# Layer 1 of a two-layer decoder on one core: the second half's norms made without GpSimd and over a longer stretch, its keys and values one group of heads later, the last output weights split once

## The chip, the cores and the metric

The kernel runs on one core of a Trainium2 chip. The metric is device time in microseconds (us), one whole execution of the program. Three runs of the kernel before gave 984.8 to 984.9, median 984.82 us.

A core has TensorE (PE, the matmuls; its weight loads are shown apart as PEld), VectorE (DVE), ScalarE (ACT), GpSimd (POOL) and SyncE (SP), which here only issues transfers. Each engine runs its own instructions in its own order and waits for the others by semaphores.

## The reference

Sequence 1024, width 1024, batch 1, all in float32. Layer 0 is a gated pooling mixer, which the change leaves alone. Layer 1 is attention in a sliding window of 128 positions, with 16 heads of 64 and two key/value heads; cut to what matters:

```python
shift, scale, gate = split(c_act @ ada_w + ada_b, 3)
hk = modulate(rmsnorm(x, kv_norm_g), kv_shift, kv_scale)   # norm for keys and values
kv = hk @ w_kv
h  = modulate(rmsnorm(x, norm_g), shift, scale)            # norm for queries and gates
q, z = split(h @ w_in, 2)
# 128 queries against 256 keys (the block before and their own)
s = q*64**-0.5 @ k + pos_bias ; s = where(band mask, s, -1e30)
m = maximum(max(s), sink) ; p = exp(s - m)
p = p / (sum(p) + exp(sink - m)) ; o = p @ v
x = x + gate * ((o * silu(z)) @ w_out)
return rmsnorm(x, final_g)
```

with `modulate(h, shift, scale) = h * (1 + scale) + shift`.

## The kernel before

**Numbers.** A float32 product is made of three matmul passes on a faster 32-bit type: each operand is split into a high part (a cast) and a low part (value minus high part), and PE adds hi x hi, lo x hi and hi x lo (lines L203 to L205). A tile of weights, 128x1024 values in 512 KB, is loaded on SP's queue into `raw`, cast by ScalarE (`wh`, L121) and subtracted by VectorE (`wl`, L123).

**Layout.** The activations `x` stay in SBUF as eight tiles (k = 0 to 7) of 128 features by 1024 positions. Everything of layer 1 is done for the first half of the positions (q = 0, 512 columns) and then for the second (q = 1). The 16 heads are four groups of four (r = 0 to 3).

**One block.** `attend(q, r, b)` handles 128 positions of one group; this is called a block here, and there are 32. In order: scores on PE into `ps_S`; VectorE copies the key-mask part (L1107), adds the bias and takes the maximum (L1111), ScalarE takes the exponential (L1115), VectorE the reciprocal `den` (L1118) and the division of `pt` (L1119); PE transposes `pt` into `ps_tp` (L1125); ScalarE and VectorE split the result into `cur` (VectorE's part is L1129); GpSimd makes `prev` (L1134) and `cur` (L1137) out of it by masking; PE multiplies with the values into `ps_o` (L1148, L1149); ScalarE's `ol` and VectorE's `of` (L1155) join its halves, VectorE multiplies the gate `szb` in (`of`, L1159), and ScalarE and VectorE (L1161) split the product into the tile `qt`, in the place where the queries were.

**The other work of a group.** `project` makes the queries (`qt`, VectorE's part L1063) and the gates (`szb`, L1077) of a group with four tiles of weights. `keys` and `values` make half a sequence's keys and values, `values_split` brings the values into position-major tiles. `out_part` multiplies one half of the heads with output weights `wbo` and adds the result to `x` (L686); after the second half of the heads the squares for the final norm are summed (`sqh`, the additions on GpSimd). For the last quarter of the work (second half of the positions, second half of the heads) `out_quarter` reads output weights that are already split: `load_last` loads four tiles, casts them on ScalarE (L1223) and takes the low part on GpSimd (L1224). The same four tiles were loaded and split in the usual way for the first half of the positions as well.

**Norms.** A norm is eight tiles of 128x512, each made as high and low part. The norms of the first half (before these stretches) use `fold_h` and `fold_l`: VectorE multiplies `x` by scale and by the row `rb` in one instruction (L892), ScalarE adds the shift and casts (`hm`), VectorE adds the shift and subtracts the high part in one instruction (L898). The norms of the second half, `hk1` for keys and values and `h11` for queries and gates, are made by `prepare` while the first half's blocks run: VectorE multiplies `x` by `rb` (`xn`, L177), ScalarE makes the high part (L159), ScalarE makes the modulated value again in full precision (L163), GpSimd subtracts (L167).

**Order.** PE's order is written out by hand. `specs` is a list of steps; a planner keeps a `clock` that grows with the cost of each matmul step, and a list of events (the parts of `attend`, the tiles of a norm, the final pass). An event is put into the program as soon as the clock has passed its due time. The due times come from the numbers `GAPS` (between blocks), `FIRST`, `LAGS` (within a block), `PREP` (between tiles of a norm) and `FINISH`. VectorE, ScalarE and GpSimd get their order from a scheduler that starts from this program order. Weights are loaded one step ahead of their use.

Of the kernel before, what the change touches and what calls it, by code (L numbers as in the profile page):

```python
# [33 lines left out]
LAGS = (6.0, 6.0)  # L34
GAPS = (6.9, 6.9, 6.6, 6.6, 6.6, 6.6, 6.6, 6.6)
FIRST = 3.2
PREP = (2.6, 4.0, 2.5)
FINISH = (1.0, 0.5)


# [15 lines left out]
def trunk(ctx, tc, xT, c, pack, ada_first, ada_rest, wu0_in, wg0_in, wa, wg, wao, wkv,  # L56
# [24 lines left out]
    def half(q):  # L81
        return slice(q * H, (q + 1) * H)
# [67 lines left out]
    def rstd_spread(rs, n):  # L150
# [3 lines left out]
            mm(bc[:, j * P:(j + 1) * P], rs[:, j:j + 1].broadcast_to([P, P]), ident,  # L154
               start=True, stop=True)
        return bc

    def mod_h(xn, a, b, h):
        nc.scalar.activation(h, xn, AF.Identity, bias=b, scale=a)  # L159

    def mod_l(xn, a, b, h, l, f_eng=None, l_eng=None):
        if f_eng is nc.scalar:
            nc.scalar.activation(xn, xn, AF.Identity, bias=b, scale=a)  # L163
        else:
            nc.vector.tensor_scalar(out=xn, in0=xn, scalar1=a, scalar2=b,
                                    op0=ALU.mult, op1=ALU.add)
        (l_eng or nc.gpsimd).tensor_sub(out=l, in0=xn, in1=h.bitcast(F32))  # L167

    def split_mod(xn, a, b, h, l, f_eng=None):

        mod_h(xn, a, b, h)
        mod_l(xn, a, b, h, l, f_eng)

    def xn_tile(k, q, rb, xn=None):
        if xn is None:
            xn = sp.tile([P, H], F32, tag="xn", name="xn", bufs=5)
        nc.vector.tensor_mul(out=xn, in0=xk[k][:, half(q)], in1=rb)  # L177
        return xn

    sqh = [None, None]  # L180

# [36 lines left out]
    with ExitStack() as sa:  # L218
# [658 lines left out]
        class Modulated:  # L877


            act = False  # L880

            def __init__(self, q, rb, a0, shift):
                self.q, self.rb, self.a0, self.shift, self.tiles = q, rb, a0, shift, []
                self.xn = {}
# [14 lines left out]
                    out=self.tiles[k // 2][:, k % 2, 1, :], in0=self.xn.pop(k), scalar=b,  # L899
                    in1=h.bitcast(F32), op0=ALU.add, op1=ALU.subtract)  # L900

            def step(self, k):
                self.step_h(k)
                self.step_l(k)

            def args(self, k):
                a, b = self.a0 + k, self.shift + k
                return acol[:, a:a + 1], adac[:, b:b + 1], self.tiles[k // 2][:, k % 2, 0, :]

            def step_h(self, k, xn=None):  # L910
                if k % 2 == 0:
                    self.tiles.append(hp.tile([P, 2, 2, H], F32R, tag="h", name="hm"))
                self.xn[k] = xn_tile(k, self.q, self.rb, xn)
                mod_h(self.xn[k], *self.args(k))

            def step_l(self, k, l_eng=None):
                mod_l(self.xn.pop(k), *self.args(k), self.tiles[k // 2][:, k % 2, 1, :],
                      nc.scalar if self.act else None,
                      l_eng)

            def __call__(self, k, i, q=0):
                return self.tiles[k // 2][:, k % 2, i, :]
# [91 lines left out]
    def keys(q, hk, ps=None):  # L1014
        def done(ps):
            cols = half(q)
            for kv in range(2):
                a, b = slice(kv * 64, kv * 64 + 64), slice((1 - kv) * 64, (1 - kv) * 64 + 64)
                nc.scalar.copy(out=KH[kv][a, cols], in_=ps[a, :])
                nc.scalar.copy(out=KH[kv][b, cols], in_=ps[a, :])  # L1020
                hs = KH[kv][a, cols].bitcast(F32)
                nc.vector.tensor_sub(out=KL[kv][a, cols], in0=ps[a, :], in1=hs)
                nc.vector.tensor_sub(out=KL[kv][b, cols], in0=ps[a, :], in1=hs)
        if ps is not None:
            return done(ps)
        return wkv[0], lambda w: gemm_steps(w, 0, hk, KT, done)
# [3 lines left out]
    def values(q, hk, ps=None):  # L1030
        def done(ps):
            vts[q] = bp.tile([P, H], F32, tag="ol", name="vt", bufs=1)
            nc.scalar.copy(out=vts[q], in_=ps)
        if ps is not None:
            return done(ps)
        return wkv[1], lambda w: gemm_steps(w, 0, hk, KT, done)

    def values_split(q):
        def run(w):
            ps = bank("d")  # L1040
            for j in range(4):
                nc.tensor.transpose(ps[:, j * P:(j + 1) * P], vts[q][:, j * P:(j + 1) * P], ident)
            pv = ps.rearrange("p (s c) -> p s c", c=64)
            vh, vl = VS[:, q * 8:q * 8 + 8, 0, :], VS[:, q * 8:q * 8 + 8, 1, :]
            nc.scalar.copy(out=vh, in_=pv)
            nc.vector.tensor_sub(out=vl, in0=pv, in1=vh.bitcast(F32))
            yield 0.43
        return None, run
# [3 lines left out]
    def queries(q, r, j, h1):  # L1052
        def run(w):
            if j == 0:
                pool, tag, bufs = (bp, "q2", 2) if r < 2 else (hp, "h", 8)
                qts[q, r] = pool.tile([P, 2, 2, H], F32R, tag=tag, name="qt", bufs=bufs)
            qt = qts[q, r]

            def done(ps):
                for e in range(2):  # L1060
                    a, b = slice(e * 64, e * 64 + 64), slice((1 - e) * 64, (1 - e) * 64 + 64)
                    nc.scalar.activation(qt[a, j, e, :], ps[a, :], AF.Copy, scale=0.125)
                    nc.vector.scalar_tensor_tensor(  # L1063
                        out=qt[b, j, e, :], in0=ps[a, :], scalar=0.125,
                        in1=qt[a, j, e, :].bitcast(F32), op0=ALU.mult, op1=ALU.subtract)
            yield from gemm_steps(w, 0, h1, KT, done)
        return wb[2 * r + j], run
# [98 lines left out]
    def out_part(q, part, n2):  # L1166

        def run(w):
            acts = lambda k, i: qts[q, 2 * part + k // 2][:, k % 2, i, :]
            for i in range(2):  # L1170
                n = 2 * n2 + i

                def done(ps):
                    residual(n, q, ps, 40)
                    if part == 1:
                        square_add(n, q, nc.gpsimd)
                yield from gemm_steps(w, i * 512, acts, 4, done)
        return wbo[part, n2], run

    def bare(f):  # L1180
        def run(w):
            f()
            yield 0.1
        return None, run
# [30 lines left out]

    last_w = []

    def load_last():

        raw = wp.tile([P, 1024], F32, tag="raw", name="raw")  # L1220
        nc.sync.dma_start(raw, wbo[1, len(last_w)])
        w = hp.tile([P, 2, T], F32R, tag="h", name="wo")
        nc.scalar.copy(out=w[:, 0, :], in_=raw)  # L1223
        nc.gpsimd.tensor_sub(out=w[:, 1, :], in0=raw, in1=w[:, 0, :].bitcast(F32))  # L1224
        last_w.append((w[:, 0, :], w[:, 1, :]))

    def stats_quarter(c):
        def f():
# [36 lines left out]
    def stats(q):  # L1265
        def f():
            state["rs"] = rstd_stats(sqh[q], 4)
        return bare(f)
# [34 lines left out]
    def prepare(m, ks, gap):  # L1303

        def gen():
            if m.rb is None:
                m.rb, m.act = state["rb"], True
            for k in ks:
                m.step(k)
                yield gap  # L1310

        return bare(lambda: push(clock[0], gen()))
# [9 lines left out]
    def project(q, r, h1, gap, after_first=()):  # L1322
        return [queries(q, r, 0, h1), *after_first, queries(q, r, 1, h1), start(q, r, gap),
                gates(q, r, 0, h1), gates(q, r, 1, h1)]

    def project_out(q, part):
        return [ready(q, part)] + [out_part(q, part, n2) for n2 in range(4)]

    def woven(l, at):

        r = []
        for i, x in enumerate(l):
            r.append(x)
            if i in at:
                r.append(bare(load_last))
        return r

    keys(0, hk0, got["pswk"])
    values(0, hk0, got["pswv"])
    specs = [  # L1340
        *project(0, 0, h10, GAPS[0], [values_split(0), stats(1)]),
        bare(norm_second), prepare(hk1, range(8), PREP[0]),
        *project(0, 1, h10, GAPS[1]),
        keys(1, hk1), values(1, hk1),
        *project(0, 2, h10, GAPS[2], [values_split(1)]),
        prepare(h11, range(4), PREP[1]),
        *project(0, 3, h10, GAPS[3]),
        prepare(h11, range(4, 8), PREP[2]),
        *project_out(0, 0),
        *project(1, 0, h11, GAPS[4]),  # L1350
        *project(1, 1, h11, GAPS[5]),
        *project(1, 2, h11, GAPS[6]),
        *project(1, 3, h11, GAPS[7]),
        *woven(project_out(0, 1) + project_out(1, 0)[:2], (0, 2, 4, 6)),
        stats(0), project_out(1, 0)[2], finish(0, 4, FINISH[0]),
        *project_out(1, 0)[3:],
        ready(1, 1),
        *[out_quarter(0, n2) for n2 in range(4)],
        out_quarter(1, 0), stats_quarter(0), out_quarter(1, 1), finish(H, 2, FINISH[1]),
# [3 lines left out]
    with tc.manual_schedule(engines={mybir.EngineType.PE}):  # L1363
        srcs = [i for i, sp_ in enumerate(specs) if sp_[0] is not None]
        loaded = {srcs[0]: got["wq"]}
        for i, (src, run) in enumerate(specs):
            if src is not None:
                nxt = srcs.index(i) + 1
                if nxt < len(srcs):
                    loaded[srcs[nxt]] = load_w(specs[srcs[nxt]][0])  # L1370
            for cost in run(loaded.pop(i, None)):
                clock[0] += cost
                while events and events[0][0] <= clock[0]:
                    advance()
        while events:
            advance()
# [55 lines left out]
```

## Time and profile before

| profiled execution | |
|---|---|
| its own time, span | 984.87 us, 982.6 us |
| instructions | 12696 |
| mean granted TensorE clock | 0.996 |
| PE | 961.9 us busy, 98% of the span |
| PEld | 801.2 us, 82% |
| VectorE | 775.7 us, 79% |
| ScalarE | 458.1 us, 47% |
| GpSimd | 145.0 us, 15% |
| HBM read, written | 111.22 MB, 13.63 MB |

The span is the time from the first to the last instruction of the profiled execution, 2.3 us less than the execution's own time. PE's load of weights overlaps its matmuls, so the two shares don't add. Layer 1 with the attention runs from about 616 us to the end; the blocks of the first half of the positions and the norms of the second half lie between about 630 and 752 us.

### The profile page before, as it was taken

Reading aid. Unit: us, or ns where it says so; the run is one execution under the profiler, and the core shown is the slowest. Engines: PE = TensorE matmul, PEld = TensorE weight load, DVE = VectorE, ACT = ScalarE, POOL = GpSimd, SP = SyncE. Lnnn points to the kernel's source line nnn. Section 1 sums busy time; section 2 is a strip of 40 time slices with the busy share of each in tenths; the row PEclk is TensorE's granted clock in tenths of the full one; section 3 lists DMA queues with packets and bytes.
Section 4 is the critical chain, followed back from the end, with each engine's and each line's share of the span. In section 5 each row is a group of like instructions: output and inputs, shape, how many; then the busy total and the mean of one; then the engine's idle time right before and its main releaser. Section 6 shows DMA issues by size and latency. Waiting matters only on the chain.

```text
span 982.6 us, 12696 instructions
## 1 busy us (share of the span) xinstructions
PE 961.9 (98%) x4538; PEld 801.2 (82%) x4538; DVE 775.7 (79%) x1411; ACT 458.1 (47%) x902; POOL 145.0 (15%) x173
## 2 busy tenths in 40 slices
PE   8999999999999999999999999999999999999996
PEld 6788888888888887888888888877888888887786
DVE  5897978677978699676782278599899878889985
ACT  6534434333433244551111145486677546566544
POOL 2100000000000000000000000052324313335723
PEclk9999999999999999999999999999999999999998
DMA  9453622264225411779861223222211221223222
GB/s 331 183 174 114 192 103 65 78 201 150 65 85 194 150 64 57 262 267 327 305 216 65 86 64 130 86 65 69 82 66 64 87 86 65 64 88 106 86 87 86
DMA packets 40625, 125.67 MB, mean 128 GB/s; under 512 B 4465, under 2 KB 6641, under 8 KB 40434
## 3 DMA queue, kind: packets, MB, share of 16 engines
q1 hardware_dynamic: 40416, 123.82, 37.6%
q10 hardware_dynamic: 146, 1.05, 0.3%
q8 instruction: 35, 0.57, 0.2%
q14 instruction: 28, 0.23, 0.1%
HBM read 111.22 MB, written 13.63 MB: 127 GB/s over the span
## 4 chain that ended last, share of the span: by engine, by line
PE 78%; DVE 16%; issue 2%; ACT 2%; POOL 1%; DMA 0%; POOLq 0%; DVEq 0%; SPq 0%; ACTq 0%
PE ps_d L214 14%; PE ps_S L214 9%; PE ps_d L636 9%; PE ps_d L203 6%; PE ps_d L204 6%; PE ps_d L205 6%; PE ps_S L636 4%; PE ps_o L214 4%; PE ps_tp L214 3%; DVE wl L123 2%; PE ps_d L374 2%; PE ps_o L636 2%; PE ps_tp L636 2%; DVE tmp L542 2%; PE ps_tp L1125 1%
## 5 line engine op out<-in xcount | busy, mean ns | idle before, releaser
L121 ACT CAST wh<-raw 128x1024 fp32r<-128x1024 f32 x73 | 76.5, 1048 | 101.4 <-PE ps_d L214 78.5
L123 DVE TENSOR_TENSOR wl<-raw,wh 128x1024 fp32r<-128x1024 f32 x73 | 94.2, 1290 | 26.7 <-ACT wh L121 22.8
L203 PE MATMUL ps_d<-hm,wh 128*128 128x512 f32 x288 | 113.8, 395 | 0.0
L205 PE MATMUL ps_d<-hm,wl 128*128 128x512 f32 x288 | 112.4, 390 | 0.3 <-DVE wl L123 0.3
L204 PE MATMUL ps_d<-hm,wh 128*128 128x512 f32 x288 | 112.4, 390 | 0.0
L239 DVE CUSTOM_DVE_ANT_0 tmp<-tmp,cact,pk 128x1024 f32<-128x1024 f32 x48 | 60.7, 1282 | 33.2 <-DMA tmp<-ada_rest 32.9
L214 PE MATMUL ps_d<-gh,wh 128*128 128x512 f32 x224 | 82.0, 389 | 0.0
L214 PE MATMUL ps_S<-gh,wh 128*128 128x512 f32 x192 | 64.5, 390 | 0.0
L205 PEld LDWEIGHTS ps_d<-hm,wl 128*128 128x128 f32 x288 | 54.1, 188 | 12.6 <-DVE wl L123 1.1
L636 PE MATMUL ps_d<-hs,ws 128*128 128x512 f32 x264 | 63.4, 389 | 0.0
L1115 ACT ACTIVATE pt<-pt,nm 128x129 f32<-128x129 f32 x128 | 50.2, 394 | 26.8 <-DVE nm L1111 24.6
L203 PEld LDWEIGHTS ps_d<-hm,wh 128*128 128x128 f32 x288 | 54.1, 188 | 10.2
L204 PEld LDWEIGHTS ps_d<-hm,wh 128*128 128x128 f32 x288 | 54.2, 188 | 10.0
L636 PEld LDWEIGHTS ps_d<-hs,ws 128*128 128x128 f32 x264 | 49.5, 188 | 10.3
L542 DVE TENSOR_TENSOR tmp<-tmp 128x1039 f32<-128x1039 f32 (+3 forms) x40 | 49.4, 1235 | 6.8 <-ACT tmp L672 5.7
L612 ACT CAST ws<-tw 128x512 fp32r<-128x512 f32 x44 | 26.8, 621 | 53.9 <-PE ps_tp L214 15.1
L636 PE MATMUL ps_d<-ha,ws 128*128 128x512 f32 x216 | 51.9, 389 | 0.0
L534 POOL MEMSET tmp<- 128x16 f32 x16 | 1.7, 111 | 331.4 <-DVE tmp L542 115.9
L214 PEld LDWEIGHTS ps_d<-gh,wh 128*128 128x128 f32 x224 | 42.1, 188 | 8.7
L636 PEld LDWEIGHTS ps_d<-ha,ws 128*128 128x128 f32 x216 | 40.5, 188 | 8.4
L147 POOL TENSOR_TENSOR rs<-v,mhalf 128x4 f32<-128x4 f32 (+1 forms) x7 | 8.2, 1164 | 241.6 <-DVE v L145 241.6
L214 PE MATMUL ps_d<-gh,wl 128*128 128x512 f32 x112 | 43.6, 389 | 0.0
(294 smaller groups left out, 2492.0 us busy)
## 6 DMA issues: line engine op xcount, KB each, us to landing
tmp<-ada_rest SPq DMA_DIRECT2D x48, 512.0 KB, 4.7
raw<-wb SPq DMA_DIRECT2D x32, 512.0 KB, 3.3
raw<-wa SPq DMA_DIRECT2D x28, 512.0 KB, 3.7
raw<-wao SPq DMA_DIRECT2D x20, 512.0 KB, 4.1
ad<-ada_first SPq DMA_DIRECT2D x16, 512.0 KB, 5.0
x<-xT SPq DMA_DIRECT2D x32, 256.0 KB, 5.9
raw<-wbo SPq DMA_DIRECT2D x16, 512.0 KB, 3.3
kept_g<-tmp SPq DMA_DIRECT2D x14, 512.0 KB, 2.9
```

The costliest lines, as they stand in the source:

```text
L121: nc.scalar.copy(out=wh, in_=raw)
L123: nc.vector.tensor_sub(out=wl, in0=raw, in1=wh.bitcast(F32))
L203: mm(ps, lh, acts(k, 0), start=k == 0, stop=False)
L204: mm(ps, lh, acts(k, 1), start=False, stop=False)
L205: mm(ps, ll, acts(k, 0), start=False, stop=k == n - 1)
L214: mm(p, lhs, acts(k, hl, q), start=start and k == 0 and s == 0, stop=stop and k == n - 1 and s == 2)
L239: nc.vector.tensor_tensor_reduce(out=raw, in0=raw, in1=ca, scale=0.5, scalar=pk[:, bcol:bcol + 1], op0=ALU.mult, op1=ALU.add, accum_out=ad ...
L374: mm(psu[i, q], w0[k // 2][:, k % 2, w, i * P:(i + 1) * P], block(k, q)[hl], start=k == 0 and s == 0, stop=k == KT - 1 and s == 2)
L542: nc.vector.tensor_add(out=nx[:, 2 * s - 1:], in0=cur[:, 2 * s - 1:], in1=cur[:, s - 1:PAD + T - s])
L612: nc.scalar.copy(out=ws[i][:, 0, :], in_=src)
L636: mm(ps, lhs, acts(k, hl), start=start and k == 0 and s == 0, stop=k == 3 and s == 2, skip_group_check=True)
L1115: nc.scalar.activation(pt[:, i, :P + 1], pt[:, i, :P + 1], AF.Exp, bias=nm[:, i:i + 1], scale=-1.0, accum_out=den[:, i:i + 1])
```

## The change

It has four parts.

1. `prepare` uses `fold_h` and `fold_l` for `hk1` and `h11`: two VectorE instructions and one ScalarE instruction a tile, instead of one of VectorE, two of ScalarE and one of GpSimd. The 16 tiles of the two norms are spread further apart: `PREP` goes from (2.6, 4.0, 2.5) to (4.8, 4.2, 4.2) us, and `h11` is cut into tiles 0 to 5 and 6 to 7 instead of 0 to 3 and 4 to 7.
2. `keys(1)` and `values(1)` stand behind the projection of group 2 and no longer ahead of it, `values_split(1)` in the projection of group 3. The pool `q2` has three buffers, and the queries of the first half's group 2 lie in it rather than in `h`.
3. `load_last` goes. The second set of output weights is loaded and split once (`load_any`, VectorE's subtraction L1188), for the first half of the positions, and kept for `out_quarter`. Sixteen loads of output weights become twelve.
4. The order of the late steps: the first tile of the second half's first output projection comes ahead of the first half's second output projection (before: behind it), `stats(0)` behind the second of these tiles (before: the first) and `finish` of the first half behind the third (before: the second).

```diff
-PREP = (2.6, 4.0, 2.5)
+PREP = (4.8, 4.2, 4.2)
...
     def queries(q, r, j, h1):
-                pool, tag, bufs = (bp, "q2", 2) if r < 2 else (hp, "h", 8)
+                pool, tag, bufs = (bp, "q2", 3) if r < 2 + (q == 0) else (hp, "h", 8)
...
-    def load_last():
-
-        raw = wp.tile([P, 1024], F32, tag="raw", name="raw")
-        nc.sync.dma_start(raw, wbo[1, len(last_w)])
+    def load_any(src):
+
+        if not isinstance(src, tuple):
+            return load_w(src)
+        raw, = fetch(wbo[src])
+        if src[0] == 0:
+            return split_w(raw)
         w = hp.tile([P, 2, T], F32R, tag="h", name="wo")
         nc.scalar.copy(out=w[:, 0, :], in_=raw)
-        nc.gpsimd.tensor_sub(out=w[:, 1, :], in0=raw, in1=w[:, 0, :].bitcast(F32))
+        nc.vector.tensor_sub(out=w[:, 1, :], in0=raw, in1=w[:, 0, :].bitcast(F32))
         last_w.append((w[:, 0, :], w[:, 1, :]))
+        return last_w[-1]
...
     def prepare(m, ks, gap):
             for k in ks:
-                m.step(k)
+                m.fold_h(k, sp.tile([P, H], F32, tag="xn", name="xn", bufs=5))
+                m.fold_l(k)
                 yield gap
...
         *project(0, 1, h10, GAPS[1]),
+        *project(0, 2, h10, GAPS[2]),
         keys(1, hk1), values(1, hk1),
-        *project(0, 2, h10, GAPS[2], [values_split(1)]),
-        prepare(h11, range(4), PREP[1]),
-        *project(0, 3, h10, GAPS[3]),
-        prepare(h11, range(4, 8), PREP[2]),
+        prepare(h11, range(6), PREP[1]),
+        *project(0, 3, h10, GAPS[3], [values_split(1)]),
+        prepare(h11, range(6, 8), PREP[2]),
...
-        *woven(project_out(0, 1) + project_out(1, 0)[:2], (0, 2, 4, 6)),
-        stats(0), project_out(1, 0)[2], finish(0, 4, FINISH[0]),
-        *project_out(1, 0)[3:],
+        *project_out(1, 0)[:2],
+        *project_out(0, 1),
+        project_out(1, 0)[2], stats(0), project_out(1, 0)[3], finish(0, 4, FINISH[0]),
+        project_out(1, 0)[4],
```

Three places show how the instructions stand on their engines. In the rows stand line, operation, output and inputs, and shape; a row that occurs several times in a stretch has xN. Lines behind the change are some 40 lower.

VectorE at the second block of the first half, where the norm `hk1` begins; before, then after:

```order
L1118 RECIPROCAL den<-den 128x4
L177 TENSOR_TENSOR xn<-x,rb_4917 128x512
L1119 TENSOR_TENSOR pt<-pt,den 128x4x128
L177 TENSOR_TENSOR xn<-x,rb_4917 128x512 x4
L1063 SCALAR_TENSOR_TENSOR qt<-ps_d,qt 64x512
L177 TENSOR_TENSOR xn<-x,rb_4917 128x512 x2
L123 TENSOR_TENSOR wl<-raw,wh 128x1024
```

```order
L1079 RECIPROCAL den<-den 128x4
L868 SCALAR_TENSOR_TENSOR xn<-x,acol,rb_4917 128x512
L1080 TENSOR_TENSOR pt<-pt,den 128x4x128
L868 SCALAR_TENSOR_TENSOR xn<-x,acol,rb_4917 128x512
L874 SCALAR_TENSOR_TENSOR hm<-xn,adac,hm 128x512
L868 SCALAR_TENSOR_TENSOR xn<-x,acol,rb_4917 128x512
L874 SCALAR_TENSOR_TENSOR hm<-xn,adac,hm 128x512
L123 TENSOR_TENSOR wl<-raw,wh 128x1024
```

Seven multiplies stood between the first division and the next split; now five folds stand there, three first folds (L868) and two second folds (L874), and the other tiles follow in later blocks.

VectorE at the end of a block while the norm `h11` is made: `of` joins and gates a block's output, `cur` is the split that GpSimd's masks start from, `qt` the split of the gated output; before, then after:

```order
L1155 SCALAR_TENSOR_TENSOR of<-ps_o,ol 64x256 x2
L1129 TENSOR_TENSOR cur<-ps_tp,cur 128x512
L1159 TENSOR_TENSOR of<-of,szb 128x256
L1107 COPY_PREDICATED ps_S<-tri,ps_S 128x2x128 x2
L1161 TENSOR_TENSOR qt<-of,qt 128x2x128
```

```order
L1116 SCALAR_TENSOR_TENSOR of<-ps_o,ol 64x256 x2
L1090 TENSOR_TENSOR cur<-ps_tp,cur 128x512
L1120 TENSOR_TENSOR of<-of,szb 128x256
L874 SCALAR_TENSOR_TENSOR hm<-xn,adac,hm 128x512
L1122 TENSOR_TENSOR qt<-of,qt 128x2x128
```

A second fold (L874) now stands right behind the gated `of`, ahead of the split into `qt`.

VectorE late in the second half, where the kept output weights are split; before, then after:

```order
L1129 TENSOR_TENSOR cur<-ps_tp,cur 128x512
L1118 RECIPROCAL den<-den 128x4
L1119 TENSOR_TENSOR pt<-pt,den 128x4x128
L123 TENSOR_TENSOR wl<-raw,wh 128x1024
L1077 SCALAR_TENSOR_TENSOR szb<-szb,ps_d 128x512
```

```order
L1090 TENSOR_TENSOR cur<-ps_tp,cur 128x512
L1188 TENSOR_TENSOR wo<-raw,wo 128x1024
L1079 RECIPROCAL den<-den 128x4
L1038 SCALAR_TENSOR_TENSOR szb<-szb,ps_d 128x512
L1080 TENSOR_TENSOR pt<-pt,den 128x4x128
L123 TENSOR_TENSOR wl<-raw,wh 128x1024
```

The first of the four kept splits (L1188) and the gate row (`szb`) moved ahead of the block's division.

More of the change, by code (lines that the diff above doesn't have):

```diff
@@ L156, in rstd_spread @@
         return bc
[L158 to L178, printed above, removed]
     sqh = [None, None]
@@ L877, in trunk @@
         class Modulated:
-            act = False
             def __init__(self, q, rb, a0, shift):
@@ L900, in fold_l @@
                     in1=h.bitcast(F32), op0=ALU.add, op1=ALU.subtract)
-            def step(self, k):
-                self.step_h(k)
-                self.step_l(k)
             def args(self, k):
@@ L908, in args @@
                 return acol[:, a:a + 1], adac[:, b:b + 1], self.tiles[k // 2][:, k % 2, 0, :]
[L910 to L919, printed above, removed]
             def __call__(self, k, i, q=0):
@@ L1177, in run @@
                 yield from gemm_steps(w, i * 512, acts, 4, done)
-        return wbo[part, n2], run
+        return (part, n2), run
     def bare(f):
@@ L1306, in gen @@
             if m.rb is None:
-                m.rb, m.act = state["rb"], True
+                m.rb = state["rb"]
             for k in ks:
-                m.step(k)
+                m.fold_h(k, sp.tile([P, H], F32, tag="xn", name="xn", bufs=5))
+                m.fold_l(k)
                 yield gap
@@ L1327, in project_out @@
         return [ready(q, part)] + [out_part(q, part, n2) for n2 in range(4)]
[L1329 to L1336, printed above, removed]
     keys(0, hk0, got["pswk"])
@@ L1369, in trunk @@
                 if nxt < len(srcs):
-                    loaded[srcs[nxt]] = load_w(specs[srcs[nxt]][0])
+                    loaded[srcs[nxt]] = load_any(specs[srcs[nxt]][0])
             for cost in run(loaded.pop(i, None)):
```

## Prediction

> **What bounds the kernel now.** I read the page first, then the waits of TensorE, then busy time by stretch, then the rows round each stall. On the page:
>
> ```profile
> span 982.6 us, 12696 instructions
> PE 961.9 (98%) x4538; PEld 801.2 (82%) x4538; DVE 775.7 (79%) x1411; ACT 458.1 (47%) x902; POOL 145.0 (15%) x173
> ```
>
> TensorE is busy for 98% of the span, and the change removes no matmul: its order on PE has the same instructions, some shifted by a few places. What can be won is PE's idle time in layer 1. The waits of PE at 600 to 760 us and at 870 to 945 us (in all, times, longest), two answers:
>
> ```profile
> PE ps_tp L1125 <- DVE pt L1119: 3.8, 3, 1.6
> ...
> PE ps_tp L1125 <- DVE pt L1119: 2.3, 2, 1.5
> PE ps_tp L154 <- DVE cur L1129: 0.4, 1, 0.4
> ```
>
> Nearly all of it is one wait: the transposes of the probabilities (L1125) wait for VectorE's division of them (L1119). Busy time by stretch (PE, PEld, DVE, ACT, POOL, granted clock, DMA share, GB/s):
>
> ```profile
> 616.00:945.00 329.00, 321.72 (x1612) 269.21 (x1611) 287.55 (x687) 207.27 (x495) 122.26 (x114) 1.00 0.24 78
> 641.00:752.00 111.00, 106.80 (x533) 88.60 (x532) 102.89 (x247) 84.99 (x192) 48.54 (x45) 1.00 0.22 71
> 645.00:669.00 24.00, 20.75 (x108) 17.16 (x105) 23.61 (x49) 20.94 (x44) 16.15 (x14) 1.00 0.21 67
> 760.00:860.00 100.00, 100.00 (x500) 84.42 (x499) 82.91 (x208) 56.43 (x143) 26.00 (x30) 1.00 0.23 74
> 878.00:934.00 56.00, 53.19 (x270) 43.92 (x269) 52.16 (x112) 32.94 (x78) 38.06 (x30) 1.00 0.30 95
> ```
>
> Over all heads PE is idle 329.0 - 321.7 = 7.3 us: 4.2 in the first stretch (641 to 752, where the second half's norms run), 2.8 in the second (878 to 934, where the output weights are split), none in the quiet 760 to 860. Even a change that cured everything would win about 7.3 us, 0.7%. PE stalls where VectorE is full: at 645 to 669 us it is idle 0.4 us of 24.
>
> **How far VectorE is ahead.** The division and the transposes after it, at the second block of heads (641) and where the two stretches end and begin:
>
> ```profile
> 640.48 0.68 DVE L1119 TENSOR_TENSOR pt<-pt,den 128x512 f32<-128x512 f32 x1
> 644.74 0.27 PE L1125 MATMUL ps_tp<-ident,pt 128*128 128x128 f32 x1
> 655.50 0.68 DVE L1119 TENSOR_TENSOR pt<-pt,den 128x512 f32<-128x512 f32 x1
> 656.33 0.63 PE L1125 MATMUL ps_tp<-ident,pt 128*128 128x128 f32 x4 [1.60 <-DVE pt L1119]
> 752.88 0.27 PE L1125 MATMUL ps_tp<-ident,pt 128*128 128x128 f32 x1
> 869.65 0.69 DVE L1119 TENSOR_TENSOR pt<-pt,den 128x512 f32<-128x512 f32 x1
> 872.51 0.27 PE L1125 MATMUL ps_tp<-ident,pt 128*128 128x128 f32 x1
> 877.77 1.19 DVE L1119 TENSOR_TENSOR pt<-pt,den 128x512 f32<-128x512 f32 x1
> 879.80 0.27 PE L1125 MATMUL ps_tp<-ident,pt 128*128 128x128 f32 x1
> ```
>
> VectorE enters the first stretch 644.74 - 641.16 = 3.6 us ahead; one block later it has none left and PE waits 1.60. From 644.74 to 752.88 PE takes 108.1 us, of which 4.2 are idle: 103.9 is the floor there.
>
> **The change, part 1: norms off GpSimd.** For each of 16 tiles the VectorE multiply (L177) becomes a fold with a scalar, the ScalarE pass L163 and the GpSimd subtract L167 go, and a second VectorE fold comes in. Price of a fold, from the first half's norms, which are written so already, with a plain 128x512 multiply-like row ahead:
>
> ```profile
> 592.53 0.68 DVE L195 TENSOR_TENSOR sqh<-sqh,sq 128x512 f32<-128x512 f32 x1
> 593.14 0.75 DVE L898 SCALAR_TENSOR_TENSOR hm<-tmp,adac,hm 128x512 fp32r<-128x512 f32 x1
> 593.80 0.75 DVE L892 SCALAR_TENSOR_TENSOR tmp<-x,acol,rb 128x512 f32<-128x512 f32 x1
> 594.46 0.74 DVE L898 SCALAR_TENSOR_TENSOR hm<-tmp,adac,hm 128x512 fp32r<-128x512 f32 x1
> ```
>
> Start to start a fold takes 0.66 us and a plain one 0.61. In the stretch stand 15 of the first kind and 16 of the second: 16 x 0.66 + 15 x 0.05 = 11.4 us more for VectorE. Against it stands what GpSimd's subtracts cost VectorE by stretching its rows; groups of 641 to 752, then the same forms in the quiet 760 to 860:
>
> ```profile
> L123 DVE TENSOR_TENSOR wl<-raw,wh 128x1024 fp32r<-128x1024 f32 x14 | 19.4, 1384 | 0.7 <-ACT wh L121 0.5
> L177 DVE TENSOR_TENSOR xn<-x,rb 128x512 f32<-128x512 f32 x15 | 11.8, 819 | 0.4 <-POOL hm L167 0.3
> L1119 DVE TENSOR_TENSOR pt<-pt,den 128x512 f32<-128x512 f32 x12 | 9.0, 747 | 0.2
> L1159 DVE TENSOR_TENSOR of<-of,szb 128x256 f32<-128x256 f32 x11 | 6.3, 569 | 0.1
> ...
> L123 DVE TENSOR_TENSOR wl<-raw,wh 128x1024 fp32r<-128x1024 f32 x15 | 18.8, 1252 | 5.4 <-ACT wh L121 3.5 <-PE ps_o L1149 1.7
> L1119 DVE TENSOR_TENSOR pt<-pt,den 128x512 f32<-128x512 f32 x11 | 7.6, 691 | 0.3
> L1161 DVE TENSOR_TENSOR qt<-of,qt 128x256 fp32r<-128x256 f32 x10 | 5.7, 572 | 0.5 <-ACT qt L1160 0.5
> L1159 DVE TENSOR_TENSOR of<-of,szb 128x256 f32<-128x256 f32 x10 | 4.2, 418 | 0.1
> ```
>
> 14 x 0.132 + 15 x 0.139 (819 against the 680 of L195) + 12 x 0.056 + 11 x 0.151 = 1.8 + 2.1 + 0.7 + 1.7 = 6.3 us, which should go. So VectorE needs 102.9 - 6.3 + 11.4 = 108.0 us, and 1.8 more for idle time that even a full VectorE keeps (0.39 of 24 at 645 to 669, 1.6%): 109.8. Starting 3.6 ahead and ending 0.15 before the transposes (as at 656.18 and 656.33 above), PE gets from the second block to the thirteenth in 109.8 - 3.6 + 0.15 = 106.4 us instead of 108.1: -1.7, if nothing new collides. That is still 2.5 above PE's floor: VectorE, not PE, sets the pace there. Spreading the norms does not help that sum, since it is VectorE's total over 110 us; it only moves the worst block.
>
> **The new collision.** GpSimd keeps two masks per block (prev and cur, L1134 and L1137), which start when VectorE has written cur. A fold can now fall into them, because in the new order a fold stands right behind "of". The trace has this once, at the end:
>
> ```profile
> 943.57 0.41 DVE L1159 TENSOR_TENSOR of<-of,szb 128x256 f32<-128x256 f32 x1
> 943.73 1.21 POOL L1134 TENSOR_SCALAR_AFFINE_SELECT prev<-cur 128x1024 fp32r<-128x1024 f32 x1 [7.50 <-DVE cur L1129]
> 943.90 1.58 DVE L1246 SCALAR_TENSOR_TENSOR x<-x,pk,rbf 128x512 f32<-128x512 f32 x1
> 945.01 1.43 POOL L1137 TENSOR_SCALAR_AFFINE_SELECT cur<-cur 128x1024 fp32r<-128x1024 f32 x1
> 945.40 1.30 DVE L1161 TENSOR_TENSOR qt<-of,qt 128x256 fp32r<-128x256 f32 x1
> ```
>
> The fold-like row waits for the first mask (1.58 instead of 0.75: +0.83) and the next split for the second (1.30 instead of 0.57: +0.73): 1.6 us a time. The new order has that sequence twice within the stretch (3.1 us) and three places where a fold or "of" can meet the second mask's end (0.4 each by the half of 0.83). Bounds 0 and 4.4; I take 3.1, the exact repeats. The first stretch then comes to -1.7 + 3.1 = +1.4, between -1.7 and +2.7, with 1 us more either way for the idle share.
>
> [...]
>
> ScalarE loses 16 passes and GpSimd 16 subtracts; neither is named by PE's waits above, so I cost this at nothing: VectorE's load covers it.
>
> **Part 2: keys and values a group later.** Their two gemms, the transposes and four VectorE splits move behind the third group of heads, and the two loads on SP's queue move past four others. The second half's keys are first read by the scores behind the first output projection, seven blocks later, and the DMA share in the stretch is 0.22: nothing waits for them, 0. Bounds: a gain of at most one of PE's smaller stalls (0.4), and as much lost, within what the ends below hold. Their VectorE work stays within the stretch and is in its sum.
>
> **Part 3: last weights split once.** Four loads of 512 KB, four ScalarE casts and GpSimd's four subtracts go; VectorE's split count stays, four of them writing the kept tile. GpSimd's subtracts held up VectorE:
>
> ```profile
> 908.83 2.41 POOL L1224 TENSOR_TENSOR wo<-raw,wo 128x1024 fp32r<-128x1024 f32 x1 [2.10 <-ACT wo L1223]
> 910.26 2.07 DVE L123 TENSOR_TENSOR wl<-raw,wh 128x1024 fp32r<-128x1024 f32 x1 [0.85 <-ACT wh L121]
> 923.34 2.38 POOL L1224 TENSOR_TENSOR wo<-raw,wo 128x1024 fp32r<-128x1024 f32 x1
> 923.58 2.42 DVE L1159 TENSOR_TENSOR of<-of,szb 128x256 f32<-128x256 f32 x1
> ```
>
> "of" took 2.42 instead of 0.42, wl 2.07 instead of 1.25: 2.8 us in two of the four. That is as much as PE's whole idle time there (2.8). But the new order puts a wo split and a gate row ahead of the division at 877 us. They take 1.2 and 0.6 us of VectorE, where PE has 2.2 us of lead at 872.51 (870.34 to 872.51) and 0.8 at 879.80: about half a microsecond of new wait, and as much again two blocks on, where two more wo splits stand. Gain 2.8 - 0.9 = 1.9, between 1.0 and 2.8.
>
> **Sum.** +1.4 - 1.9 = -0.5 us. The profiled execution took 984.87 us (span 982.6 and 2.3 around it), the median of the runs is 984.82. So 984.4.
>
> **Rivals.** Faster: the folds get in ahead of the masks, and the second stretch clears. With 0.8 us of collisions and 2.3 gained: -1.7 + 0.8 - 2.3 = -3.2, 981.7; for it, that "of" behind cur is never delayed by prev in the quiet rows (418 ns). Against it, the row of 1.58.
>
> Slower: VectorE becomes the bound of the first stretch outright, with every collision paid (4.4), 1 us more idle share and 1.0 won later: -1.7 + 4.4 + 1.0 - 1.0 = +2.7, 987.6. For it: VectorE's 0.4 us of idle time in the 24 of the worst blocks. Against it: the quiet stretch, where VectorE has 17 us of 100 to spare and PE never waits, as it will again behind the thirteenth block. It decides once collisions and idle share together pass 1.7 + 1.9 + 2.0 = 5.6 us.
>
> No relief from GpSimd at all: VectorE keeps the 6.3 us and gains 11.4 of work: 102.9 + 11.4 + 1.8 - 3.4 = 112.7 against 108.1, +4.6, and with nothing won later 989.5. The rows of 2.07 and 2.42 beside GpSimd's speak against it. [...]
>
> That the norms are not in fact spread out is ruled out by the built order, where the 16 second folds stand behind nine different blocks.
>
> **How the numbers follow.** A change under 0.2% (2.0 us) can't be told from none. My forecast, both effects cancelling to within that, 0.47 (its own range 983.0 to 986.8); the faster rival 0.32; the slower one 0.17, no relief 0.04. The ends worked out above are 984.9 - 1.7 - 2.8 = 980.4 and 987.6; leaving a tenth out at each side, 981.2 to 987.4. Faster 0.32, same 0.47, slower 0.21.
>
> **What would show it.** In the new profile: folds at 0.75 us except for one or two near 1.6 between "of" and the split; VectorE busy over 97% from 641 to 752; PE waiting for the division there 4 to 7 us, spread over more blocks than three; under 1.5 us at 870 to 945. I am wrong if VectorE has idle time in the first stretch, or if PE waits there for something else than the division, such as ScalarE's pass between the two folds.

## The result, and the profile after

The changed kernel took 993.81 us (median of 6 runs, 992.0 to 997.1) beside 984.86 for the kernel before (6 runs): ratio 1.0087, 95% interval 1.0075 to 1.0099. It is 9 us slower; the forecast was 984.4, in a range from 981.2 to 987.4, and its chance of slower was 0.21.

The page of the changed kernel, profiled execution 992.01 us:

```profile
span 990.3 us, 12652 instructions
PE 965.1 (97%) x4538; PEld 804.0 (81%) x4538; DVE 778.0 (79%) x1427; ACT 442.8 (45%) x882; POOL 111.0 (11%) x153
```

The engines' totals look as forecast: GpSimd 34 us less, ScalarE 15 us less, VectorE 2.3 us more, the same matmuls. PE is busy for 3.2 us longer with the same 4538 matmuls, so some of them ran slower. The waits of PE at 641 to 764 us (in all, times, longest):

```profile
PE ps_S L1066 <- DVE ps_S L1062: 5.5, 1, 5.5
PE ps_tp L1086 <- DVE pt L1080: 2.5, 2, 2.0
PE ps_d L183 <- DVE wl L123: 1.3, 1, 1.3
PE ps_tp L1086 <- ACT hm L870: 0.4, 1, 0.4
```

The division (L1080), on which the whole forecast rested, costs 2.5 us, less than the 3.8 of before. The long wait is another: the scores (L1066) of one block wait 5.5 us for L1062. That is the fill of the scores' left half with -1e30, which only the first block of each group needs, since there is no block of keys before it. Busy time by stretch (PE, PEld, DVE, ACT, POOL, granted clock as a share of full speed, DMA share, GB/s):

```profile
616.00:945.00 329.00, 317.51 (x1573) 266.02 (x1572) 282.87 (x692) 190.10 (x471) 86.22 (x93) 0.98 0.21 68
641.00:762.00 121.00, 111.21 (x535) 92.30 (x534) 113.44 (x266) 74.02 (x176) 25.47 (x29) 0.96 0.21 66
645.00:669.00 24.00, 24.00 (x125) 20.38 (x124) 23.26 (x55) 15.91 (x37) 7.49 (x9) 1.00 0.20 67
735.00:740.00 5.00, 5.00 (x22) 4.22 (x21) 3.65 (x10) 1.45 (x3) 2.49 (x3) 0.66 0.16 64
750.00:756.00 6.00, 4.36 (x14) 3.86 (x15) 4.90 (x15) 2.43 (x9) 0.90 (x1) 0.50 0.00 0
887.00:943.00 56.00, 54.57 (x278) 45.52 (x277) 48.61 (x117) 30.73 (x79) 28.24 (x26) 1.00 0.18 57
```

At 645 to 669 us PE no longer waits at all (3.25 of 24 us before). But the granted clock, 1.00 in every such stretch before, is 0.66 just behind the wait of 2.04 us and 0.50 at the end of the wait of 5.55 us and behind it. What VectorE and GpSimd did at the long one:

```profile
746.56 0.84 DVE L1116 SCALAR_TENSOR_TENSOR of<-ps_o,ol 64x256 f32<-64x256 f32 x2
747.43 0.69 DVE L1090 TENSOR_TENSOR cur<-ps_tp,cur 128x512 fp32r<-128x512 f32 x1
748.04 0.41 DVE L1120 TENSOR_TENSOR of<-of,szb 128x256 f32<-128x256 f32 x1
748.20 1.21 POOL L1095 TENSOR_SCALAR_AFFINE_SELECT prev<-cur 128x1024 fp32r<-128x1024 f32 x1 [1.50 <-DVE cur L1090]
748.37 1.58 DVE L874 SCALAR_TENSOR_TENSOR hm<-xn,adac,hm 128x512 fp32r<-128x512 f32 x1
749.47 1.43 POOL L1098 TENSOR_SCALAR_AFFINE_SELECT cur<-cur 128x1024 fp32r<-128x1024 f32 x1
749.87 1.30 DVE L1122 TENSOR_TENSOR qt<-of,qt 128x256 fp32r<-128x256 f32 x1
751.23 0.55 DVE L1062 MEMSET ps_S<- 128x256 f32 x2
751.64 0.44 PE L1066 MATMUL ps_S<-KH,qt 128*128 128x128 f32 x1 [5.55 <-DVE ps_S L1062]
753.92 0.63 PE L182 MATMUL ps_d<-qt,wh 128*128 128x512 f32 x1
754.35 0.63 PE L183 MATMUL ps_d<-qt,wl 128*128 128x512 f32 x1
```

The two fills are the last of a queue: behind the gated `of`, a second fold that takes 1.58 us beside GpSimd's first mask (0.75 at 754.12), and a split that takes 1.30 beside the second (0.57 in the quiet stretch of before). PE, whose order is fixed, stands at the fills' scores from 746.1 us. Behind the wait its 512-column matmuls start 0.43 us apart instead of 0.23. In the kernel before the same two fills (L1101) stood round the division of the preceding block:

```profile
740.89 0.27 DVE L1101 MEMSET ps_S<- 128x256 f32 x1
741.07 0.16 DVE L1118 RECIPROCAL den<-den 128x4 f32<-128x4 f32 x1
741.28 0.27 DVE L1101 MEMSET ps_S<- 128x256 f32 x1
741.46 0.73 DVE L1119 TENSOR_TENSOR pt<-pt,den 128x512 f32<-128x512 f32 x1
```

Below, time between blocks is the difference of the starts of their first transposes (L1125, L1086 after), and blocks are numbered from 1 (the expectations below number them from 0, so their block 10 is block 11 here). For blocks 2 to 13 (the first stretch) these are 644.74 and 752.88 before, 108.1 us; the changed kernel's are these, 117.6 us:

```profile
645.00 0.60 PE L1086 MATMUL ps_tp<-ident,pt 128*128 128x128 f32 x4
762.58 0.60 PE L1086 MATMUL ps_tp<-ident,pt 128*128 128x128 f32 x4
```

So the first stretch is 9.4 us longer, and all of it is lost at its end. What the changed kernel wins up to block 5, 2.3 us, it has given back by block 11, where the two are level (89.7 us from block 2 after, 89.9 before). The last two intervals, 9.16 and 9.09 us before, are these after, 1.6 and 8.0 us longer:

```profile
734.74:745.50 10.76, 10.76 (x47) 8.94 (x48) 8.95 (x24) 5.04 (x14) 2.49 (x3) 0.84 0.26 88
745.50:762.58 17.08, 11.53 (x47) 9.57 (x46) 13.57 (x28) 5.12 (x13) 3.17 (x3) 0.80 0.10 34
```

In the first of them PE has no idle time at all, only a lower clock; in the second stands the wait of 5.55 us. The second stretch, from block 25 to block 32, is 1.2 us shorter (67.5 against 68.7).

### The profile page after: what moved, and what is told of

The parts are those of the page before. It is cut to its first block, busy times and chain, and to the rows that moved or that the text cites. A ratio compares the mean times of both kernels' runs of the same rounds, so it can differ in the third digit from the quotient of the medians.

```text
span 990.3 us, 12652 instructions
## 1 busy us (share of the span) xinstructions
PE 965.1 (97%) x4538; PEld 804.0 (81%) x4538; DVE 778.0 (79%) x1427; ACT 442.8 (45%) x882; POOL 111.0 (11%) x153
## 4 chain that ended last, share of the span: by engine, by line
PE 77%; DVE 16%; ACT 3%; issue 2%; POOL 1%; DMA 1%; POOLq 0%; DVEq 0%; SPq 0%; ACTq 0%
PE ps_d L192 14%; PE ps_S L192 9%; PE ps_d L614 9%; PE ps_d L181 6%; PE ps_d L182 6%; PE ps_d L183 6%; PE ps_S L614 4%; PE ps_o L192 4%; PE ps_tp L192 3%; DVE wl L123 2%; PE ps_d L352 2%; PE ps_o L614 2%; PE ps_tp L614 2%; DVE tmp L520 2%; DVE pt L1072 1%
## 5 line engine op out<-in xcount | busy, mean ns | idle before, releaser
L121 ACT CAST wh<-raw 128x1024 fp32r<-128x1024 f32 x69 | 72.4, 1049 | 100.0 <-PE ps_d L192 73.0
L123 DVE TENSOR_TENSOR wl<-raw,wh 128x1024 fp32r<-128x1024 f32 x69 | 85.5, 1239 | 23.8 <-ACT wh L121 20.1
L192 PEld LDWEIGHTS ps_S<-gh,wh 128*128 128x128 f32 x192 | 35.9, 188 | 7.4
L1095 POOL TENSOR_SCALAR_AFFINE_SELECT prev<-cur 128x1024 fp32r<-128x1024 f32 x28 | 34.2, 1220 | 61.7 <-DVE cur L1090 60.9
```

Source lines behind the costliest of these rows:

```text
L121: nc.scalar.copy(out=wh, in_=raw)
L123: nc.vector.tensor_sub(out=wl, in0=raw, in1=wh.bitcast(F32))
L192: mm(p, lhs, acts(k, hl, q), start=start and k == 0 and s == 0, stop=stop and k == n - 1 and s == 2)
L1095: nc.gpsimd.affine_select(out=v8(prev), in_=v8(cur).bitcast(F32), pattern=[[0, 8], [-1, P]], base=-1, channel_multiplier=1, compare_op=ALU ...
```

## Experiments

Two theories to begin with. Theory 1: one late row, the fill, costs the time. Theory 2: VectorE is the bound of the first stretch, and the fill is only where it shows this time. All ratios are to the kernel before, run beside it on the same chip, where its median was 986.04 us (984.74 beside i, k and l). A stretch is read from one profiled execution, and those lie up to 3 us from their medians: 1.9 to 2.5 us above in a, b and x, 1.8 and 2.9 below in the changed kernel and in o.

**a_zero_first.** The changed kernel with precedence for the fill of group 3's first block:

```diff
-            if b == 0:
+            with tc.high_priority() if b == 0 and r == 3 else nullcontext():
-                nc.vector.memset(s[:, :, :P], NEG)
+                b == 0 and nc.vector.memset(s[:, :, :P], NEG)
```

> The changed kernel, but the two rows that fill the scores of group 3's first block (L1062) are given precedence, so that VectorE does them before that block's predecessor is divided, and not behind the fold and the split of the output. Theory 1 (one late row): TensorE's idle 5.55 us at 746.1 to 751.6 us goes, and with it the stretch at a granted clock of 0.50 behind it (750 to 756, 3.0 us of full speed): 993.8 - 5.6 - 3.0 = 985.2, between 984 and 988, granted clock back to 0.994 or more. Theory 2 (VectorE's load): VectorE has the same work in the same stretch, so the wait comes back at the divisions of the next blocks: 991 to 994.

986.56 us, ratio 1.0017 (1.0005 to 1.0029). The fills ran at 743.48 and 745.13 us, ahead of the division, and PE's wait for them was gone:

```profile
743.48 0.27 DVE L1062 MEMSET ps_S<- 128x256 f32 x1
745.13 0.27 DVE L1062 MEMSET ps_S<- 128x256 f32 x1
```

```profile
PE ps_tp L1086 <- DVE pt L1080: 4.2, 3, 2.0
PE ps_d L183 <- DVE wl L123: 1.3, 1, 1.3
PE ps_tp L1086 <- ACT hm L870: 0.4, 1, 0.4
```

The fold of 1.58 us and a split of 1.31 stand there as before (at 751.11 and 752.62 us); only PE no longer waits behind them. The waits for the division went from 2.5 to 4.2 us: 1.6 us came back at the division of the same block, as theory 2 has it, but not more. The first stretch is 111.4 us. Of the 0.87% some 0.70% hung on this one pair of rows.

**b_zero_late.** The converse: the kernel before with nothing but that pair put behind the split of the last output written.

```diff
+            with tc.issue_after(last_qt[-1]) if b == 0 and r == 3 else nullcontext():
+                b == 0 and nc.vector.memset(s[:, :, :P], NEG)
...
-        nc.vector.tensor_sub(out=qt[:, :, 1, cols], in0=of,
+        last_qt.append(nc.vector.tensor_sub(out=qt[:, :, 1, cols], in0=of,
```

> The kernel before, with nothing moved but the two rows that fill the scores of group 3's first block: they stand behind the split of an earlier block's output, as the changed kernel has them, and no longer round the division. Theory 1: they start at about 749.3 us instead of 740.9, TensorE has nothing else from about 744.4 us, so it idles about 5 us and then runs 3 us short of full clock: 984.9 + 8 = 993, between 989 and 995. Theory 2: VectorE has nothing more to do than before: 985 to 986.

993.11 us, ratio 1.0084 (1.0066 to 1.0101), as slow as the whole change; VectorE has no instruction more. Its wait, and the stretch behind it, at half clock again:

```profile
PE ps_S L1105 <- DVE ps_S L1101: 5.4, 1, 5.4
```

```profile
752.00:757.00 5.00, 4.68 (x15) 4.13 (x16) 2.52 (x13) 1.77 (x8) 2.04 (x2) 0.50 0.00 0
```

The first stretch is 116.5 us, 8.4 more than before: 5.45 of idle time and about 2.9 of slow matmuls.

**c_weights_once.** Parts 3 and 4 alone, on the kernel before: `load_any` for `load_last`, and the later order of steps.

> The kernel before with the third and fourth part alone: last output weights split once, and the late order of output projections. Both theories: the trace of the changed kernel is 1.2 us shorter from block 12 to block 31 and 0.8 us shorter behind it, so 984.9 - 2.0 = 982.9, between 982 and 984. If the gain belongs to other parts: 984.9.

983.98 us, ratio 0.9983 (0.9971 to 0.9994): 1.7 us won where 2.0 were expected. From block 25 to 32 it takes 67.4 us (68.7 before), with one wait for the division there, of 1.7 us. The 0.8 us behind block 32 that I had counted on are not shown: PE's named waits there are 1.9 us or more in all kernels, and the time varies from 40.6 to 41.9 us in those with the two parts and from 40.9 to 41.4 in those without.

**d_folds_only.** The folds alone, in the old spacing and order:

```diff
-                m.step(k)
+                m.fold_h(k, sp.tile([P, H], F32, tag="xn", name="xn", bufs=5))
+                m.fold_l(k)
```

> The kernel before with the folds alone: norms without GpSimd, at the old spacing, keys and values where they were. In its order the two filling rows stand round the division, as before. Theory 1: VectorE has about 5 us more to do and some stalls of 1 to 2 us more, but no long one: 985 to 988. Theory 2: VectorE's load is packed still closer than in the changed kernel, so this is at least as slow: 993 or more.

991.48 us, ratio 1.0066 (1.0051 to 1.0082): outside what theory 1 expected, and under the 993 of theory 2. I had looked at the fills of group 3 only. Here those of group 1 were late, behind the same rows, `of`, fold of 1.58, split of 1.30:

```profile
668.37 1.58 DVE L898 SCALAR_TENSOR_TENSOR hm<-xn,adac,hm 128x512 fp32r<-128x512 f32 x1
669.88 1.30 DVE L1161 TENSOR_TENSOR qt<-of,qt 128x256 fp32r<-128x256 f32 x1
671.23 0.55 DVE L1101 MEMSET ps_S<- 128x256 f32 x2
```

**i_folds_first.** The same with precedence for the fills of groups 1 to 3.

> The kernel before with the folds alone (as d_folds_only), and the filling rows of the first block of groups 1, 2 and 3 given precedence on VectorE. Theory 1 (one late row): d_folds_only lost 4.86 us at 666.8 to 671.7 us to the filling rows of group 1, and some 2.5 us of half clock behind it; both go: 991.5 - 7.4 = 984.1, between 982.5 and 986.5, or within 0.2% of the kernel before. Theory 2 (VectorE's load, 5 us more than before): 989 or more.

989.99 us, ratio 1.0056 (1.0044 to 1.0069). Theory 1 alone falls here. The fill was early, and PE waited further on, for the norm that the keys read:

```profile
PE ps_d L203 <- ACT hm L894: 4.2, 1, 4.2
PE ps_tp L1125 <- DVE pt L1119: 1.2, 3, 0.6
```

With folds at the old spacing VectorE, without a gap from 664 to 677 us, doesn't deliver the tile in time: this is theory 2. The changed kernel, with wider spacing and later keys, doesn't have this wait. Whether another order on VectorE would have been enough was not tried.

**k_spread_weights and l_half_folds.** Parts 2 to 4 and the new spacing, with the norms' subtractions on GpSimd as before (k), and with folds for the first of the two norms only (l); fills first in both.

```diff
+                if m is h11:
+                    m.step(k)
+                else:
+                    m.fold_h(k, sp.tile([P, H], F32, tag="xn", name="xn", bufs=5))
+                    m.fold_l(k)
```

> The kernel before with the second, third and fourth part (later keys and values, last weights once, late order) and the wider spacing of the norms, but the norms' subtractions still on GpSimd, and the filling rows first. If the two waits of 1.6 us at 656 and 667 us come from the burst of seven multiplies at the start of the norms, they shrink as in the changed kernel (2.3 us from block 1 to block 4): 2.0 + 2.3 us under the kernel before, 0.4% faster. If spreading only moves GpSimd's subtractions under the masks of the later blocks, the later blocks give it back: 0.2% faster, as c_weights_once.

> As k_spread_weights, but the first of the two norms (keys and values) by folds on VectorE, the second with GpSimd's subtractions. If the folds' extra VectorE work can be borne in the first blocks and not in the last (the changed kernel wins 2.3 us from block 1 to 4 and loses 4.4 us from block 8 to 12 with the filling rows first): 0.4 to 0.5% faster than the kernel before. If half the folds cost half of the loss: 0.2% faster or less.

k: 984.72 us, ratio 0.9999 (0.9990 to 1.0008), slower than both of its expectations. l: 982.81 us, ratio 0.9980 (0.9971 to 0.9988), with c the fastest here. The first stretch is 108.5 us in k and 107.5 in l, against 111.4 in a_zero_first, which differs from l in that stretch by the folds of the second norm (and by precedence for one group's fill instead of three): these cost 3.8 us, those of the first win 0.9. Of the 3.8 us 1.7 are slow matmuls behind a wait of 2.05 us, which those of k (2.10) and l (1.73) in the same place escaped. Both keep a wait of about 2 us at 734 to 736 us, ahead of block 11, which the changed kernel and a_zero_first have too; the five kernels with early keys and values (before, b, c, d, i) wait 0.5 us at most in that place:

```profile
736.20 0.41 PE L1125 MATMUL ps_tp<-ident,pt 128*128 128x128 f32 x2 [2.10 <-DVE pt L1119]
```

**p_first_vt_apart and o_half_vt_apart.** A third theory for that wait: the values that wait for their transposes (`vt`) hold the one buffer that the blocks' `ol` needs.

```diff
-            vts[q] = bp.tile([P, H], F32, tag="ol", name="vt", bufs=1)
+            vts[q] = sp.tile([P, H], F32, tag="xn", name="vt", bufs=5)
```

> As a_zero_first, but the values that wait for their transpose (vt) lie in a buffer of the pool xn and no longer in the one buffer that each block's ol needs. Theory 3 (one buffer): in the changed kernel vt holds it from 713.8 to 718.7 us, so the ol of a block whose output is done at 713.5 starts at 720.5, two blocks' ends fall on VectorE together, and the division of block 10 is 2.04 us late. With vt apart that wait and the 1 to 2 us of half clock behind it go: 0.2 to 0.35% under a_zero_first, 983 to 985. Rival (VectorE's total over the stretch sets the pace): the wait turns up at another block, within 0.1% of a_zero_first, 986 to 987.

> As l_half_folds, with vt apart in the same way. Theory 3: its wait of 1.73 us at block 10 goes: 0.35 to 0.4% faster than the kernel before (l_half_folds: 0.2%). Rival: the same as l_half_folds.

990.46 us, ratio 1.0048 (1.0035 to 1.0061), and 987.99 us, ratio 1.0021 (1.0006 to 1.0036): both slower than without it, and outside what either side expected. (The runs of o lie in two groups, 984.5 to 986.9 and 989.1 to 990.8 us; the profiled one is of the first.) That the buffer costs the time falls. The wait at block 11 shrank to 1.1 and 0.7 us, so the buffer had a part in that wait, but longer ones stood before and behind it, 3.8 us at 759 us in p and 4.0 us at 725 us in o. Waits of the division in p:

```profile
PE ps_tp L1086 <- DVE pt L1080: 6.5, 3, 3.8
```

**w_pinned_first and x_folds_pinned.** The multiplies (w, on c) or first folds (x, on a) held in the written order on VectorE, fills first.

```diff
-        nc.vector.tensor_mul(out=xn, in0=xk[k][:, half(q)], in1=rb)
+        tc.keep_in_program_order(nc.vector.tensor_mul(out=xn, in0=xk[k][:, half(q)], in1=rb))
```

> c_weights_once (last weights once, norms with GpSimd as before), with the norms' multiplies (L177) held in the written order on VectorE, so that they come two at a time and not seven at the second block, and the filling rows first. If the two waits of 1.6 us at 656 and 667 us come from that burst, they shrink to under 0.5 us each: 2 us under c_weights_once, 0.35 to 0.45% faster than the kernel before. If they come from GpSimd's subtractions, which stay: as c_weights_once, 0.2%.

> a_zero_first with the first folds of the norms held in the written order on VectorE (and the filling rows of all groups first). If what is left of the loss (3.3 us from block 1 to block 12) comes from folds that the scheduler put ahead of divisions, it shrinks: 0.2% or more under a_zero_first, 983 to 985. If it is VectorE's total load in blocks 5 to 12, which no order changes: 986 to 988.

997.73 us, ratio 1.0118 (1.0102 to 1.0133), and 990.76 us, ratio 1.0055 (1.0040 to 1.0069). Both are slower than either side expected. The burst of multiplies at the second block costs two waits, but it also has the norm ready for the keys: held back in w, PE waited for the norm instead:

```profile
PE ps_tp L1125 <- DVE pt L1119: 4.1, 3, 1.7
PE ps_d L203 <- ACT hm L159: 3.0, 1, 3.0
PE ps_d L204 <- POOL hm L167: 2.7, 2, 1.7
```

In x the waits for the division became longer (7.1 us against 4.2 in a). It does not show that order can't help; it shows that this one doesn't.

## Why the prediction was wrong

**What was right.** The terms of the first stretch came out near their sizes. These are VectorE's groups of 641 to 762 us after the change:

```profile
L123 DVE TENSOR_TENSOR wl<-raw,wh 128x1024 fp32r<-128x1024 f32 x15 | 18.2, 1216 | 0.2
L874 DVE SCALAR_TENSOR_TENSOR hm<-xn,adac,hm 128x512 fp32r<-128x512 f32 x16 | 13.7, 861 | 0.0
L868 DVE SCALAR_TENSOR_TENSOR xn<-x,acol,rb 128x512 f32<-128x512 f32 x15 | 10.7, 726 | 0.0
L1080 DVE TENSOR_TENSOR pt<-pt,den 128x512 f32<-128x512 f32 x12 | 8.2, 685 | 0.2
```

- Relief from GpSimd: `wl` 1384 to 1216 ns, `pt` 747 to 685, and the stretched multiplies are gone. 14 x 0.168 + 12 x 0.062 + 2.1 is 5.2 us, and the gated `of` (569 to 484 ns, 11 times) adds 0.9; 6.3 was forecast. The rival without relief is out.
- The folds took 0.73 and 0.75 us, as priced, apart from the collisions. (The 11.4 us for them adds up to 11.3.)
- The collision: 16 x (861 - 750) is 1.8 us on second folds, with the splits behind them (643 against 572 ns, 11 times) 2.6 us, and the 1.58 and 1.30 of the row that I had found came back digit for digit. 3.1 was forecast. No run shows the lower bound of 0: in i_folds_first a fold ahead of the gated `of` took 0.75 us (at 669.07), but the `of` behind it 1.31, where it took 0.41 a block earlier.
- With the fill out of the way, a_zero_first stands at ratio 1.0017, inside the forecast's range; its first stretch is +3.3 us where +1.4 was forecast (from -1.7 to +2.7, and 1 more either way). VectorE is busy there for 107.2 us; the sum had 108.0 + 3.1 less the 3.6 that it is ahead, 107.5. But it is idle for 4.2 us where 1.8 was put, 2.0 of them in the interval with the slow matmuls, from block 11 to 12.
- Of the signs that the text named, the two folds near 1.6 us and the waits at 870 to 945 us (1.3) came as said. VectorE was busy for 106.85 of the 111 us from 641 to 752, 96% where over 97 was named, and PE waited 2.5 us for the division where 4 to 7 were.

**The step that failed** is the sum for the first stretch. It took VectorE's total for PE's pace and let PE wait for one thing, the division. PE waits on VectorE for several kinds of row, each with its own due time: the fills, the weights' low parts, the norms' tiles. The built order had the fill behind the fold and the split. I priced the fold and its collisions there and overlooked that PE's next matmul hung on the row behind them. a and b show it from both sides: taking the row ahead wins 0.70% of the 0.87, putting it behind costs the kernel before 0.84%. The text named this as what would make it wrong ("if PE waits there for something else than the division"), but no rival carried it, so no range did.

**A second term was missing:** a wait was priced at its length. With the 5.55 us came a granted clock of 0.50 (row 750 to 756), and after the 2.04 us one of 0.66 over 735 to 740. The 9.4 us are 5.6 of additional idle time of PE and 4.1 lost to slow matmuls (2.4 behind the long wait, 1.7 behind the other), less 0.2. In the kernel before no wait in the attention was above 1.65 us, and the clock stayed at 1.00, so its trace showed no such price there. The clock also accounts for the scatter of the changed kernel: its run with a clock of 0.992 spans 990.3 us, the one with 0.987 spans 995.4. The clock not granted is 0.008 x 990.3 = 7.9 and 0.013 x 995.4 = 12.9 us, a difference of 5.0, and the spans differ by 5.1.

**Part 2, costed at nothing,** or the new spacing, which no run has apart from it, brings the wait at block 11 (2.04 us), outside the 0.4 that bounded part 2. In k the whole of the spacing and part 2 comes to +0.3 us in the first stretch: what the early blocks win is lost at block 11. Why that block is late is open; the buffer is at most a part of it.

**Part 3 was right in kind and too large:** -1.9 forecast (1.0 to 2.8 won), -1.2 to -1.3 measured in the second stretch. Part 4, the late order, has no term in the sum; no run has part 3 without it.

The slower rival had a price of 2.7 us and, in part, the cause of the 3.3 us that are left in a_zero_first: half of them are idle time of PE, which comes with the folds of the second norm (a against l), and half the slow matmuls. But VectorE is not the bound outright that this rival made it: it is busy for 113.44 of 121 us in the changed kernel, 94%, and idle while PE runs slowly. Its limit, "once collisions and idle share together pass 5.6", counted the wrong thing; one pair of rows decided.

## What to carry to other kernels

When an engine is near full, list each row on it that another engine with a fixed order waits for, and look up in the built order what stands ahead of each, small rows first: a pair of 0.27 us fills that slid behind a fold and two splits cost 7 to 8 us here (0.70% taken away in a, 0.84% put on in b). A total of the engine's work says how much slack there is, not who gets it, and freeing one buffer or pinning one kind of row in such a stretch moved the wait or made it longer, and the kernel slower, four times out of four. Give rows that gate PE precedence explicitly instead of relying on where a scheduler leaves them, and price a long wait of PE at its length plus the slow matmuls behind it (1.7 us in the first stretch of a, 4.1 in that of the changed kernel).

## What the runs showed of the hardware

In these traces the granted clock was 0.50 behind some waits of PE, and the length of the wait alone doesn't decide it. With four waits of 4.2 to 5.6 us (d, i, b, the changed kernel) it was 0.50 from before the wait's end: for 6.83 us in the changed kernel (749.56 to 756.39), and throughout the stretches read in the others, 671 to 677 us in d, 676 to 682 in i and 752 to 757 in b. Behind waits of 2.0 to 4.0 us in the changed kernel, a, x, p, o and w (2.7) its mean was 0.72 to 0.75 over six microseconds, that is, half for about three of them: 0.75 behind the 4.0 us of o, 0.72 behind the 2.0 of the changed kernel (734.7 to 740.7). In w, behind a wait of 3.0 us and with 1.72 us more of idle time in the six microseconds from 679.4, it was 0.53. In k, with a wait of 2.10 us, it was 1.00 from 731.20 to 742. The same six microseconds, 736 to 742, in a_zero_first and then in k:

```profile
736.00:742.00 6.00, 5.14 (x22) 4.62 (x23) 4.75 (x11) 2.25 (x4) 2.50 (x3) 0.72 0.27 90
```

```profile
736.00:742.00 6.00, 5.80 (x32) 5.07 (x33) 5.50 (x14) 5.93 (x11) 2.51 (x3) 1.00 0.41 145
```

The longest waits in the attention (616 to 945 us) were 1.65 us in the kernel before and 1.7 in c, and the clock was 1.00 there in both; l, with 1.7 in the first stretch, has a mean of 0.997 over the whole program, as c has.

What a and k differ in is where the wait falls. In the changed kernel the clock went to 0.50 at 735.91 and 749.56 us and back to 1.00 at 739.32 and 756.39: these four times lie 3.41, 10.24 and 6.83 us apart, 1, 3 and 2 times 3.41. In steps of 3.41 us counted from there, PE was idle for 2.04 us in the step ahead of 735.91, for 3.41 in the one ahead of 749.56 and for 2.09 in the one behind it, and the step after each of these was at 0.50; in the other steps of the attention it was idle for 1.27 us at most, and the step after was at 1.00. In the kernel before, counted from its one change, at 974.45 us, the most in a step of the attention is 1.61 us, and all are at 1.00. The stretch of 3.41 us of a with the wait and the one behind it, then two of k:

```profile
733.69:737.10 3.41, 1.36 (x7) 0.85 (x7) 3.35 (x9) 3.33 (x8) 0.00 (x0) 1.00 0.25 68
737.10:740.51 3.41, 3.41 (x15) 3.13 (x14) 3.35 (x9) 0.59 (x1) 1.08 (x2) 0.50 0.24 93
```

```profile
731.20:734.62 3.42, 2.90 (x13) 2.06 (x11) 3.39 (x11) 3.40 (x12) 2.39 (x3) 1.00 0.01 2
734.62:738.03 3.41, 1.83 (x14) 1.82 (x15) 2.92 (x5) 3.10 (x5) 2.29 (x3) 1.00 0.49 159
```

In a PE is idle for 2.05 us in one stretch, and the next is at 0.50; in k the 2.10 us stand as 0.52 in one and 1.58 in the next, and the clock is 1.00 to 742. Where steps of k would end is not shown by a change of its clock here: 734.62 is where the author put one. A step of 3.41 us at 0.50 is 1.7 us less than full speed. In the kernel before 0.81 us of idle time, in the step from 971.04 to 974.45, stood ahead of a clock of 0.50, and 1.30 us in the step from 899.36 ahead of 1.00, so idle time in a step doesn't account for all of it.
